# Recurrence stage of a two-block model: GpSimd operations in pieces, chain products on 128 rows, in-chunk products head by turn

## The chip, the cores and the metric

The kernel runs on one core of a Trainium2 chip. The metric is the device time of one execution in microseconds (us), the median of the runs shown. TensorE does the matrix products, VectorE and ScalarE elementwise work, GpSimd elementwise work between tiles in SBUF, and SyncE issues most transfers. Each engine takes its instructions strictly in the order in which the program lists them.

## The reference, cut to what matters

The whole model has two blocks. The stage that is changed computes the recurrence of the first block, 12 heads of 64 columns over 1024 tokens:

```python
def rwkv7_step(state, inp):
    r, decay, k, v, kk, a = inp
    sa = jnp.einsum('bhij,bhj->bhi', state, -kk)
    state = (state * decay[:, :, None, :]
             + sa[..., None] * (kk * a)[:, :, None, :]
             + v[..., None] * k[:, :, None, :])
    out = jnp.einsum('bhij,bhj->bhi', state, r)
    return state, out
...
_, y = lax.scan(rwkv7_step, state0, (r, decay, k, v, kk, a))
```

Before it, `x @ w_in` gives r, k and v. After it come a per-head normalization, a gate, the product with `w_out`, a mixture of 32 experts, and the second block with its attention.

## The kernel before

The scan is done in chunks of 64 tokens. The two heads of a pair lie in partitions 0 to 63 (`lo`) and 64 to 127 (`hi`). A *unit* is one pair and half of the sequence, so there are 12 units (`NU`) of 8 chunks (`HC`). Function `phase_units` works on them with these steps for each unit:

- `project`: 24 groups of three 128x512 products (lines 103 to 105). Each weight tile is first parted into a high and a low share: `wh` by ScalarE, `wl` by GpSimd (line 458, 128x1024).
- `tokens`: elementwise work that makes `G`, `BK`, `HK`; GpSimd takes lines 588 (128x512), 603 (64x512, twice) and 611 (128x1024); VectorE's lines 591 to 608 read two SBUF tiles each.
- `within`: the in-chunk products (line 636, K=64 rows, 128 columns), first all 8 chunks of the lo head, then all 8 of the hi head. VectorE masks the lo result straight from PSUM (line 642); for the hi head ScalarE copies (645) and GpSimd masks (647).
- `solve`: 15 small pairs of VectorE operations (706: a product of two SBUF tiles, 708: its sum).
- `masks`: GpSimd, line 722, four operations of 64x512. `inverse`: products on line 735, then `T64` (line 756).
- `chain`: the recurrence over the 8 chunks, in three steps a chunk. Step one: product with `G` and `X` (777), copied to `R` (768). Step two: `T64` by `R` (782), copied into `X` (768), and the first part of the output (785). Step three: the new state (789, 791) and the second part of the output, `H` by `X` (793). Each is issued for the lo and then for the hi head. 782 and 793 use 64 rows each (64*64 in the trace), 777, 785 and 789 use 128 rows (128*64).
- `finish`: normalization on GpSimd (815 to 844), transposes on TensorE (837).

The units overlap. Table `PLAN` gives, for each step of a unit, the slot in which it is emitted, 24 slots a unit; `ORDER` orders steps within one slot. So while the chain of unit v runs, `solve`, `masks` and `inverse` of unit v+1, `tokens` and `within` of unit v+2 and `project` of unit v+3 are emitted between its steps. Nothing reorders them later: a VectorE operation that takes long delays the chain's copies that are emitted behind it.

All results of TensorE go to PSUM tiles; `pA` has three buffers, `pC` one for each tag. The product on line 103 to 105 comes as one row in the trace; an f32 product of the chain comes as two rows (two passes).

Of the kernel before, what the change touches and what calls it, by code (L numbers as in the profile page):

```python
# [142 lines left out]
def phase_lowrank(g, xh0, xl0):  # L143
# [228 lines left out]
HC = 8  # L372
# [9 lines left out]
    "masks": [-21, -20, -19, -16, -16],  # L382
    "inverse": [-8, -7, -4, -3, -2, -2, 0, 0, 0],
    "start_state": [-12],
    "within": [-35, -35, -35, -35, -35, -34, -33, -33, -32, -31, -30],
    "tokens": [-47, -47, -46, -45, -44, -44, -43, -42, -41, -41, -40, -39, -38, -37, -37, -36, -34, -33, -33, -31,
        -31, -31, -29],
    "lt_load": [-24],
# [16 lines left out]
def phase_units(g, xh, xl):  # L405
    nc, tc, a = g.nc, g.tc, g.a
    with ExitStack() as c:
        wp = c.enter_context(tc.tile_pool(name="uw", bufs=2, reuse_waits="tile"))
        hv = c.enter_context(tc.tile_pool(name="uh", bufs=2, reuse_waits="tile"))
# [10 lines left out]
        lo, hi = slice(0, 64), slice(64, 128)  # L420
# [2 lines left out]
        nc.gpsimd.memset(T16, 0.0)  # L423

        L16, L32, T16T, X2 = (sm.tile([P, HC, 2, 64], F32, name=n) for n in ("L16", "L32", "T16T", "X2"))
        for t in (L16, L32, T16T, X2):
            nc.gpsimd.memset(t, 0.0)
        EP = el.tile([P, HC, 65], F32, name="EP")
        nc.gpsimd.memset(EP[:, :, 0:1], math.exp(-M0))
# [47 lines left out]
        M = {}  # L477
# [16 lines left out]
        def msplit2(j):  # L494
            if j < 12:
                mh, ml, m = M[j]
                kn = order[j][2]
                nc.gpsimd.tensor_tensor(ml[:, :kn], m[:, :kn], mh[:, :kn].bitcast(F32), op=OP.subtract)


        swap = {(1, 1): [(oload, 0, 0)], (1, 5): [(oload, 0, 2)], (2, 1): [(osplit, 0, 0)], (2, 2): [(osplit, 0, 1)],
# [48 lines left out]
        def tokens(v):  # L550
# [34 lines left out]
            fv = f[:, v, :, None]  # L585
            nc.vector.tensor_scalar(fv, EP[:, :, 64:65], math.exp(M0), None, op0=OP.mult)
            u.G = el.tile([P, HC, 2, 64], F32, name="G", bufs=2)
            nc.gpsimd.tensor_tensor(u.G[:, :, 1, :], w4(r), EP[:, :, 1:65], op=OP.mult)
            yield
            kn = el.tile([P, 512], F32, name="kn")  # L590
            nc.vector.scalar_tensor_tensor(kn, k, pc[:, 32 + q:33 + q], sq, op0=OP.mult, op1=OP.mult)
# [8 lines left out]

            u.BK = el.tile([P, HC, 2, 64], F32, name="BK")
            for sl, o in ((lo, 0), (hi, 1)):
                nc.gpsimd.tensor_tensor(u.BK[sl, :, o, :], w4(kn)[sl], w4(EN)[sl], op=OP.mult)
                nc.vector.tensor_tensor(u.BK[sl, :, 1 - o, :], w4(al)[sl], w4(EN)[sl], op=OP.mult)
                yield

# [4 lines left out]
            nc.gpsimd.tensor_tensor(u.HK, u.BK, fv[:, :, None, :].to_broadcast([P, HC, 2, 64]), op=OP.mult)  # L611
            yield
            pb = pA.tile([P, 512], F32, name="pA")
            nc.tensor.matmul(pb, ones, bo)
# [11 lines left out]
        def within(v):  # L626

            u = U[v]
            u.M = []
            for e, sl in enumerate((lo, hi)):  # L630
                M = el.tile([P, HC, 2, 64], F32, name=f"M{e}")
                for q in range(2):
                    pl = pA.tile([P, 4, 2, 64], F32, name="pA")
                    for i in range(4):
                        cc = 4 * q + i
                        nc.tensor.matmul(pl[:, i], u.BK[sl, cc], u.G[sl, cc])
                        if i == 1:
                            yield
                    qs = slice(4 * q, 4 * q + 4)
                    mb = mk.to_broadcast([P, 4, 2, 64])  # L640
                    if e == 0:
                        nc.vector.tensor_tensor(M[:, qs], pl, mb, op=OP.mult)
                        yield
                    else:
                        nc.scalar.activation(M[:, qs], pl, AF.Copy)
                        yield
                        nc.gpsimd.tensor_tensor(M[:, qs], M[:, qs], mb, op=OP.mult)
                u.M.append(M)
# [13 lines left out]
        def hand_over(v):  # L662

            u = U[v]
            h, q = divmod(v, NPAIR)
            u.L = sm.tile([P, HC, 64], F32, name="L")
            u.H = hv.tile([P, HC, 64], F32, name="H")
            u.GA, u.GB = (hv.tile([P, HC, 2, 64], F32, name=n) for n in ("GA", "GB"))
            u.XA, u.XB = (hv.tile([P, 2, HC, 64], F32, name=n) for n in ("XA", "XB"))
            MA, MB = u.M  # L670
            for s, M in ((lo, MA), (hi, MB)):
                nc.sync.dma_start(u.L[s], M[s, :, 0, :])
            for s, o, M, G, in ((lo, hi, MA, u.GA), (hi, lo, MB, u.GB)):
                nc.sync.dma_start(G[s], u.G[s])
                nc.sync.dma_start(G[o], M[o])
                nc.sync.dma_start(u.H[s], M[s, :, 1, :])
            yield
            u.TK = []
            for e, sl in enumerate((lo, hi)):
                pk = pA.tile([P, HC, 64], F32, name="pA")  # L680
                for cc in range(HC):
                    nc.tensor.transpose(pk[:, cc, :], u.HK[sl, cc], g.ident[sl, sl])
                    if cc == 3:
                        yield
                t = hv.tile([P, HC, 64], F32, name=f"TK{e}")
# [32 lines left out]
        def masks(v):  # L718
            u = U[v]
            for e, sl in enumerate((lo, hi)):  # L720
                for t, m in ((L16, "m16"), (L32, "m32")):
                    nc.gpsimd.tensor_tensor(t[sl, :, e, :], u.L[sl], cv(g, m)[sl][:, None, :].to_broadcast([64, HC, 64]), op=OP.mult)
                    yield

        def inverse(v):
# [26 lines left out]
            yield  # L752
            ps = pA.tile([P, HC, 64], F32, name="pA")
            yield from mul(ps, X2, T32T)
            u.T64 = hv.tile([P, HC, 64], F32, name="T64")
            nc.vector.tensor_tensor(u.T64, ps, T32T, op=OP.add)
            yield

        def chain(v):
# [12 lines left out]
            for cc in range(HC):  # L772
# [7 lines left out]
                for sl, G, X, TK, tag in hd:  # L780
                    us = pC.tile([P, 64], F32, name=tag)
                    nc.tensor.matmul(us[sl], u.T64[sl, cc, :], R[sl])
                    copy(sl, X[sl, 1, cc, :], us[sl])
                for sl, G, X, TK, tag in hd:
                    nc.tensor.matmul(yy[sl], G[:, cc, 1, :], X[:, 0, cc, :], start=True, stop=False)
# [1 line left out]
                for sl, G, X, TK, tag in hd:  # L787
# [2352 lines left out]
```

## Time and profile before

| | |
|---|---|
| median of 3 runs | 3401.09 us (3397.03 to 3405.79) |
| the profiled execution | 3407.47 us, span 3405.7 us |
| busy over the span | TensorE 89%, VectorE 64%, GpSimd 46%, ScalarE 45% |
| recurrence chains of the 12 units | from 260 to 912 us of the span |
| first expert weights requested | 951 us, behind this stage |

The profile is one execution. "Idle before" in its rows is the time in which the engine had nothing to do just before an operation, and the arrow names what ended it. [...]

### The profile page before, as it was taken

To read this page: it belongs to the slowest core of one execution; us is meant where nothing else is said; L and a number is where in the kernel's file an instruction comes from. 1 tells how busy PE (TensorE), PEld (TensorE's weight loads), DVE (VectorE), ACT (ScalarE), POOL (GpSimd) and SP (SyncE) were. 2 spreads that over 40 slices of the span, in tenths; PEclk is the share of its full clock that TensorE was granted. 3 is DMA by queue.
4 is the path that set the end of the run, shared out by engine and by line. 5 is a ranking of instruction groups with operands and counts; after the bars stand their busy time and mean duration, and the time that the engine had idled before them with its cause. 6 is when DMAs were issued, how large, how long until landed. Compare 5 with 4: busy or idle time off the path is not lost. (4 is left out here: it accounts for less than half of the span.)

```text
span 3405.7 us, 47172 instructions
## 1 busy us (share of the span) xinstructions
PE 3028.9 (89%) x16804; PEld 2114.5 (62%) x16804; DVE 2175.5 (64%) x3459; ACT 1535.0 (45%) x2828; POOL 1577.0 (46%) x1301
## 2 busy tenths in 40 slices
PE   7788888888978998699988988998899889999998
PEld 4365566565666765689864555557677665555556
DVE  2157787777468987768336666766447346667665
ACT  3343343333337977533224544445445334444452
POOL 0153555555344554554115554567546314444465
PEclk8888888888978999799999999999899989999999
DMA  9744453445579999532211111146224311111136
GB/s 298 279 111 103 107 146 93 110 109 151 156 253 312 323 329 336 184 112 83 91 63 51 39 47 44 37 144 209 92 75 158 123 52 58 41 49 41 41 106 213
DMA packets 394064, 457.14 MB, mean 134 GB/s; under 512 B 123319, under 2 KB 301970, under 8 KB 393698
## 3 DMA queue, kind: packets, MB, share of 16 engines
q1 hardware_dynamic: 380032, 426.15, 40.2%
q0 software_dynamic: 7616, 17.09, 1.5%
q10 hardware_dynamic: 6178, 10.86, 0.8%
q8 instruction: 133, 2.18, 0.3%
q14 instruction: 105, 0.86, 0.1%
HBM read 329.40 MB, written 101.11 MB: 126 GB/s over the span
## 5 line engine op out<-in xcount | busy, mean ns | idle before, releaser
L2110 ACT ACTIVATE p<-st 128x512 f32<-128x512 f32 (+1 forms) x672 | 378.2, 584 | 393.7 <-PE st L2108 313.0
L2029 DVE TENSOR_REDUCE mx<-s 128x1 f32<-128x1280 f32 x256 | 380.4, 1486 | 263.1 <-PE s L2028 263.1
L2120 POOL TENSOR_TENSOR acc<-acc,p 128x512 f32<-128x512 f32 x256 | 379.4, 1482 | 131.1 <-ACT p L2110 117.8
L2128 PE MATMUL o<-p,V 128*64 128x512 f32 (+1 forms) x1344 | 318.2, 595 | 0.0
L2120 DVE TENSOR_TENSOR acc<-acc,p 128x512 f32<-128x512 f32 x256 | 284.6, 1112 | 7.6
L1412 DVE TENSOR_TENSOR wl<-wr,wh 128x1024 fp32r<-128x1024 f32 x156 | 227.8, 1487 | 41.0 <-ACT wh L1411 40.9
L103 PE MATMUL pz<-xh,wh 128*128 128x512 f32 x440 | 229.1, 521 | 11.1 <-ACT wh L452 7.6
L1411 ACT ACTIVATE wh<-wr 128x1024 fp32r<-128x1024 f32 x192 | 198.9, 1055 | 40.9 <-DMA wr<-in_exp_up_dram 16.0
L105 PE MATMUL pz<-xh,wl 128*128 128x512 f32 x440 | 188.4, 428 | 11.5 <-POOL wl L458 7.9
L104 PE MATMUL pz<-xl,wh 128*128 128x512 f32 x440 | 187.8, 427 | 0.0
L103 PE MATMUL pj<-hh,wh 128*128 128x512 f32 (+1 forms) x416 | 160.6, 386 | 9.4 <-DVE xk L2780 4.6
L2128 PEld LDWEIGHTS o<-p,V 128*64 128x64 f32 x1344 | 81.7, 136 | 140.2 <-issue 136.4
L2120 POOL TENSOR_TENSOR acc<-p 128x512 f32<-128x512 f32 (+1 forms) x40 | 48.6, 1215 | 240.4 <-ACT p L2110 240.4
L1792 POOL TENSOR_TENSOR wl<-wr,wh 128x512 fp32r<-128x512 f32 (+1 forms) x70 | 88.4, 1275 | 152.5 <-ACT wh L1790 152.2
L105 PE MATMUL pj<-hh,wl 128*128 128x512 f32 (+1 forms) x416 | 156.6, 377 | 0.5 <-POOL wl L1792 0.5
L104 PE MATMUL pj<-hl,wh 128*128 128x512 f32 (+1 forms) x416 | 156.2, 376 | 0.0
L1412 POOL TENSOR_TENSOR wl<-wr,wh 128x1024 fp32r<-128x1024 f32 x36 | 88.8, 2470 | 145.5 <-ACT wh L1411 125.7
L2108 PE MATMUL st<-QQ,K 128*128 128x512 f32 (+1 forms) x352 | 150.5, 429 | 2.8 <-ACT p L2110 2.7
L2142 POOL TENSOR_TENSOR rg<-rg,gt 128x512 f32<-128x512 f32 (+1 forms) x40 | 48.5, 1213 | 221.3 <-ACT rg L2141 221.1
L105 PE MATMUL pj<-wh,hl 128*128 128x256 f32 x480 | 142.7, 297 | 4.6 <-POOL hl L1873 4.5
L104 PE MATMUL pj<-wl,hh 128*128 128x256 f32 x480 | 141.5, 295 | 4.5 <-DVE wl L1792 4.4
L103 PE MATMUL pj<-wh,hh 128*128 128x256 f32 x480 | 142.4, 297 | 1.2 <-DVE hh L1872 1.2
(515 smaller groups left out, 8415.9 us busy)
## 6 DMA issues: line engine op xcount, KB each, us to landing
wr<-in_exp_gate_dram SPq DMA_DIRECT2D x64, 512.0 KB
wr<-in_exp_up_dram SPq DMA_DIRECT2D x64, 512.0 KB
wr<-in_exp_down_dram SPq DMA_DIRECT2D x32, 1024.0 KB
w<-in_l_w_out_dram SPq DMA_DIRECT2D x56, 512.0 KB
wm<-in_l_w_mod_dram SPq DMA_DIRECT2D x48, 512.0 KB
w<-in_w_in_dram SPq DMA_DIRECT2D x40, 512.0 KB
wr<-in_l_w_in_dram SPq DMA_DIRECT2D x33, 512.0 KB
y<-ysd SPq DMA_DIRECT2D x16, 512.0 KB
```

The lines of the kernel that those rows point to most:

```text
L103: nc.tensor.matmul(out, lh, rh, start=start, stop=False)
L104: nc.tensor.matmul(out, lh, rl, start=False, stop=False)
L105: nc.tensor.matmul(out, ll, rh, start=False, stop=stop)
L1411: nc.scalar.activation(wh, w, AF.Copy)
L1412: eng.tensor_tensor(wl, w, wh.bitcast(F32), op=OP.subtract)
L1792: eng.tensor_tensor(st["l"][:, ks], st["w"][:, ks], st["h"][:, ks].bitcast(F32), op=OP.subtract)
L2029: nc.vector.tensor_reduce(m[:, j:j + 1], ps.rearrange("p a b -> p (a b)")[:, :SK], axis=AX.X, op=OP.max)
L2108: nc.tensor.matmul(st[:, :n], kk[:, kt * P:(kt + 1) * P], qv[:, pt.q0:pt.q0 + n], start=(j == 0), stop=(j == len(passes) - 1))
L2110: nc.scalar.activation(p[:, :n], st[:, :n], AF.Exp, scale=self.scale)
L2120: eng.tensor_tensor(a, r.p[r.kts[0], e][:, :n] if r.first else a, r.p[r.kts[i], e][:, :n], op=OP.add)
L2128: nc.tensor.matmul(pt.po[64 * e:64 * e + 64, :n], pt.out["V"](e, kt), r.p[kt, e][:, :n], start=(r.first and i == 0), stop=(r.last and i == ...
L2142: nc.gpsimd.tensor_tensor(rg[:, :n], rg[:, :n], pt.gt[:, :n], op=OP.mult)
```

## The change

The diff does three things. GpSimd's operations of lines 458, 498, 588, 603, 611 and 722 are cut along the free dimension into pieces of 256 elements a partition. `T64` and `H` become tiles of both heads, 128 rows by 2x64 columns a chunk, zero outside the head's own block, so that 782 and 793 run on all 128 rows with `R` or `X` whole; `T64` is one tile for all units, `H` is two in turn, and all three are cleared once at the start of the stage. And `within` issues the in-chunk products of the two heads in turn, with a PSUM tile for each; its part of `PLAN` is shortened to the steps that are left.

```diff
-    "within": [-35, -35, -35, -35, -35, -34, -33, -33, -32, -31, -30],
+    "within": [-35, -35, -35, -34, -33, -33, -32, -30],
...
-        for t in (L16, L32, T16T, X2):
+        T64, *Hs = (sm.tile([P, HC, 2, 64], F32, name=n) for n in ("T64", "H0", "H1"))
+        for t in (L16, L32, T16T, X2, T64, *Hs):
             nc.gpsimd.memset(t, 0.0)
...
-                nc.gpsimd.tensor_tensor(wl, w, wh.bitcast(F32), op=OP.subtract)
+                for c0 in range(0, KT, 2):
+                    nc.gpsimd.tensor_tensor(wl[:, c0:c0 + 2], w[:, c0:c0 + 2], wh[:, c0:c0 + 2].bitcast(F32), op=OP.subtract)
...
-            nc.gpsimd.tensor_tensor(u.G[:, :, 1, :], w4(r), EP[:, :, 1:65], op=OP.mult)
+            for c0 in range(0, HC, 4):
+                ks = slice(c0, c0 + 4)
+                nc.gpsimd.tensor_tensor(u.G[:, ks, 1, :], w4(r)[:, ks], EP[:, ks, 1:65], op=OP.mult)
...
-            u.M = []
-            for e, sl in enumerate((lo, hi)):
-                M = el.tile([P, HC, 2, 64], F32, name=f"M{e}")
-                for q in range(2):
-                    pl = pA.tile([P, 4, 2, 64], F32, name="pA")
-                    for i in range(4):
-                        cc = 4 * q + i
-                        nc.tensor.matmul(pl[:, i], u.BK[sl, cc], u.G[sl, cc])
-                        if i == 1:
-                            yield
...
+            u.M = [el.tile([P, HC, 2, 64], F32, name=f"M{e}") for e in range(2)]
+            for q in range(2):
+                pl = [pA.tile([P, 4, 2, 64], F32, name="pA") for _ in range(2)]
+                for i in range(4):
+                    cc = 4 * q + i
+                    for e, sl in enumerate((lo, hi)):
+                        nc.tensor.matmul(pl[e][:, i], u.BK[sl, cc], u.G[sl, cc])
+                    if i == 1:
                         yield
...
-            u.H = hv.tile([P, HC, 64], F32, name="H")
+            u.H = Hs[v % 2]
...
-                nc.sync.dma_start(u.H[s], M[s, :, 1, :])
+                nc.sync.dma_start(u.H[s, :, e, :], M[s, :, 1, :])
...
-                    nc.gpsimd.tensor_tensor(t[sl, :, e, :], u.L[sl], cv(g, m)[sl][:, None, :].to_broadcast([64, HC, 64]), op=OP.mult)
+                    for c0 in range(0, HC, 4):
+                        ks = slice(c0, c0 + 4)
+                        nc.gpsimd.tensor_tensor(t[sl, ks, e, :], u.L[sl, ks], cv(g, m)[sl][:, None, :].to_broadcast([64, 4, 64]), op=OP.mult)
...
-            u.T64 = hv.tile([P, HC, 64], F32, name="T64")
-            nc.vector.tensor_tensor(u.T64, ps, T32T, op=OP.add)
+            for e, sl in enumerate((lo, hi)):
+                nc.vector.tensor_tensor(T64[sl, :, e, :], ps[sl], T32T[sl], op=OP.add)
...
-                    nc.tensor.matmul(us[sl], u.T64[sl, cc, :], R[sl])
+                    nc.tensor.matmul(us[sl], T64[:, cc, e, :], R)
...
-                    nc.tensor.matmul(yy[sl], u.H[sl, cc, :], X[sl, 1, cc, :], start=False, stop=True)
+                for e, (sl, G, X, TK, tag) in enumerate(hd):
+                    nc.tensor.matmul(yy[sl], u.H[:, cc, e, :], X[:, 1, cc, :], start=False, stop=True)
```

Lines 603 and 611 are cut in the same way. The code grows by a few lines, so that line 458 is line 460 afterwards, 722 is 729, 636 is 644, 782 is 789 and 793 is 800.

In GpSimd's queue, in a unit from the middle of the stage, these rows stand behind the first half of the normalization before (`L_1114` and `L_1115` are the masked tiles L16 and L32, the row of `Y` is the second half of the normalization):

```order
L458 TENSOR_TENSOR wl<-w,wh 128x1024
L722 TENSOR_TENSOR L_1114<-L,const_102 64x8x64
L722 TENSOR_TENSOR L_1115<-L,const_102 64x8x64
L722 TENSOR_TENSOR L_1114<-L,const_102 64x8x64
L830 TENSOR_TENSOR Y<-Y,mv 128x512
L588 TENSOR_TENSOR G<-z_3118,EP 128x8x64
L458 TENSOR_TENSOR wl<-w,wh 128x1024
L722 TENSOR_TENSOR L_1115<-L,const_102 64x8x64
```

After the change the same place reads:

```order
L460 TENSOR_TENSOR wl<-w,wh 128x256 x4
L729 TENSOR_TENSOR L_1114<-L,const_102 64x4x64 x2
L729 TENSOR_TENSOR L_1115<-L,const_102 64x4x64 x2
L729 TENSOR_TENSOR L_1114<-L,const_102 64x4x64 x2
L837 TENSOR_TENSOR Y<-Y,mv 128x512
L593 TENSOR_TENSOR G<-z_3210,EP 128x4x64 x2
L460 TENSOR_TENSOR wl<-w,wh 128x256 x4
L729 TENSOR_TENSOR L_1115<-L,const_102 64x4x64 x2
```

No operation changed its place there; seven of the eight became pieces of half or a quarter of their size.

On TensorE, the in-chunk products of a unit (`pA_3923`, `pA_3929`: lo head, `pA_3936` and the tile behind it: hi head) stand among the chain's products like this before:

```order
L636 MATMUL pA_3923<-G_3798,BK_3897 128x128 x4
L636 MATMUL pA_3929<-G_3798,BK_3897 128x128 x4
L636 MATMUL pA_3936<-G_3798,BK_3897 128x128 x2
L782 MATMUL cA_3939<-R_3908,T64_3581 64x64
L782 MATMUL cB_3942<-R_3908,T64_3581 64x64
L785 MATMUL yy_3907<-XA_3055,GA_3053 64x64
L785 MATMUL yy_3907<-XB_3056,GB_3054 64x64
L636 MATMUL pA_3936<-G_3798,BK_3897 128x128 x2
```

and like this after it (`pA_4041` and `pA_4065` lo, `pA_4042` and `pA_4066` hi):

```order
L644 MATMUL pA_4041<-G_3908,BK_4012 128x128
L644 MATMUL pA_4042<-G_3908,BK_4012 128x128
L644 MATMUL pA_4041<-G_3908,BK_4012 128x128
L644 MATMUL pA_4042<-G_3908,BK_4012 128x128
L789 MATMUL cA_4053<-R_4025,T64_1118 64x64
L789 MATMUL cB_4056<-R_4025,T64_1118 64x64
L792 MATMUL yy_4024<-XA_3144,GA_3142 64x64
L792 MATMUL yy_4024<-XB_3145,GB_3143 64x64
L644 MATMUL pA_4065<-G_3908,BK_4012 128x128
L644 MATMUL pA_4066<-G_3908,BK_4012 128x128
```

The heads now alternate, eight products instead of ten stand ahead of this chain step, and the second pair of PSUM tiles is asked for while the first pair is being emptied. The chain's own products keep their places; `T64_1118` is the one tile of all units.

## Rows read from the trace of the kernel before

**Rows 1.** Busy time by window: us, then busy (and count) of each engine, PEclk, DMA

```profile
260.00:912.00 652.00, 566.26 (x4898) 389.50 (x4898) 477.72 (x1251) 243.59 (x445) 325.26 (x312) 0.89 0.45 118
870.00:912.00 42.00, 41.90 (x381) 27.45 (x380) 20.37 (x74) 11.99 (x24) 15.94 (x19) 1.00 0.36 113
```

**Rows 2.** Idle TensorE time before L782 and before L777: us, times

```profile
  DVE R L768: 73.2, 46
...
  DVE XA L791: 98.5, 43
```

**Rows 3.** TensorE in order of time, unit around 608: start us, us, what

```profile
608.09 0.47 PE L782 MATMUL cA<-R,T 64*64 64x64 f32 x2 [3.14 <-DVE R L768]
...
610.61 0.63 PE L103 MATMUL pz<-xh,wh 128*128 128x512 f32 x1
...
615.24 0.39 PE L103 MATMUL pz<-xh,wh 128*128 128x512 f32 x1
...
625.26 0.47 PE L777 MATMUL cA<-XA,GA 128*64 128x64 f32 x2 [3.79 <-DVE XA L791]
```

**Rows 4.** VectorE in order of time, the same stretch

```profile
602.91 2.22 DVE L706 TENSOR_TENSOR pr<-Tn,LT 64x9 f32<-64x9 f32 x1
...
606.58 1.00 DVE L706 TENSOR_TENSOR pr<-Tn,LT 64x25 f32<-64x25 f32 x1
...
607.82 0.22 DVE L768 COPY R<-cA 64x64 f32<-64x64 f32 x1
...
620.05 2.92 DVE L591 SCALAR_TENSOR_TENSOR kn<-z,pcol,sq 128x512 f32<-128x512 f32 x1
622.90 1.59 DVE L706 TENSOR_TENSOR pr<-Tn,LT 64x225 f32<-64x225 f32 x1
```

**Rows 5.** GpSimd in order of time, the same stretch

```profile
602.71 2.40 POOL L458 TENSOR_TENSOR wl<-w,wh 128x1024 fp32r<-128x1024 f32 x1 [3.01 <-ACT wh L452]
605.05 3.81 POOL L722 TENSOR_TENSOR L<-L,const 64x512 f32<-64x512 f32 x3
...
620.07 2.36 POOL L458 TENSOR_TENSOR wl<-w,wh 128x1024 fp32r<-128x1024 f32 x1
```

**Rows 6.** VectorE by line and shape, 260 to 912: busy us, mean ns, idle before

```profile
L591 DVE SCALAR_TENSOR_TENSOR kn<-z,pcol,sq 128x512 f32<-128x512 f32 x10 | 24.8, 2479 | 0.0
...
L756 DVE TENSOR_TENSOR T<-pA,T32T 128x512 f32<-128x512 f32 x12 | 8.3, 692 | 1.1 <-PE pA L735 0.8
...
L595 DVE SCALAR_TENSOR_TENSOR kn<-th,kn 128x512 f32<-128x512 f32 x10 | 6.9, 692 | 0.3
...
L706 DVE TENSOR_TENSOR pr<-Tn,LT 64x4 f32<-64x4 f32 x11 | 1.7, 158 | 0.4
```

**Rows 7.** TensorE, first passes of chain products around 478 and 481

```profile
478.81 0.27 PE L782 MATMUL cA<-R,T 64*64 64x64 f32 x1
...
479.07 0.27 PE L785 MATMUL yy<-XA,GA 128*64 128x64 f32 x1
...
481.28 0.22 PE L777 MATMUL cA<-XA,GA 128*64 128x64 f32 x1
...
481.40 0.65 PE L735 MATMUL pA<-X,T16T 128*64 128x64 f32 x16
```

**Rows 8.** TensorE, the first in-chunk products of one unit

```profile
634.44 2.16 PE L636 MATMUL pA<-G,BK 64*128 64x128 f32 x20
```

**Rows 9.** GpSimd by line and shape, 260 to 912

```profile
L458 POOL TENSOR_TENSOR wl<-w,wh 128x1024 fp32r<-128x1024 f32 x26 | 61.6, 2369 | 44.1 <-ACT wh L452 41.1 <-DMA L<-M 2.9
...
L843 POOL TENSOR_TENSOR yf<-yf,fbo 128x256 f32<-128x256 f32 x22 | 17.5, 797 | 40.5 <-issue 23.1 <-ACT yf L840 17.4
...
L815 POOL TENSOR_TENSOR mv<-st 128x8 f32<-128x8 f32 x11 | 2.7, 250 | 54.4 <-DVE st L798 54.4
```

**Rows 10.** ScalarE's copy of the second head's in-chunk products

```profile
L645 ACT ACTIVATE M<-pA 128x512 f32<-128x512 f32 x20 | 11.9, 597 | 36.8 <-PE pA L636 36.6
```

**Rows 11.** GpSimd at the start of the stage: the last large clear

```profile
163.84 0.94 POOL L427 MEMSET X<- 128x1024 f32 x1
```

More of the change, by code (lines that the diff above doesn't have):

```diff
@@ L497, in msplit2 @@
                 kn = order[j][2]
-                nc.gpsimd.tensor_tensor(ml[:, :kn], m[:, :kn], mh[:, :kn].bitcast(F32), op=OP.subtract)
+                for c0 in range(0, kn, 2):
+                    nc.gpsimd.tensor_tensor(ml[:, c0:c0 + 2], m[:, c0:c0 + 2], mh[:, c0:c0 + 2].bitcast(F32), op=OP.subtract)
         swap = {(1, 1): [(oload, 0, 0)], (1, 5): [(oload, 0, 2)], (2, 1): [(osplit, 0, 0)], (2, 2): [(osplit, 0, 1)],
@@ L602, in tokens @@
             for sl, o in ((lo, 0), (hi, 1)):
-                nc.gpsimd.tensor_tensor(u.BK[sl, :, o, :], w4(kn)[sl], w4(EN)[sl], op=OP.mult)
+                for c0 in range(0, HC, 4):
+                    ks = slice(c0, c0 + 4)
+                    nc.gpsimd.tensor_tensor(u.BK[sl, ks, o, :], w4(kn)[sl, ks], w4(EN)[sl, ks], op=OP.mult)
                 nc.vector.tensor_tensor(u.BK[sl, :, 1 - o, :], w4(al)[sl], w4(EN)[sl], op=OP.mult)
@@ L610, in tokens @@
             u.HK = el.tile([P, HC, 2, 64], F32, name="HK")
-            nc.gpsimd.tensor_tensor(u.HK, u.BK, fv[:, :, None, :].to_broadcast([P, HC, 2, 64]), op=OP.mult)
+            for c0 in range(0, HC, 2):
+                ks = slice(c0, c0 + 2)
+                nc.gpsimd.tensor_tensor(u.HK[:, ks], u.BK[:, ks], fv[:, ks, None, :].to_broadcast([P, 2, 2, 64]), op=OP.mult)
             yield
@@ L628, in within @@
             u = U[v]
-            u.M = []
-            for e, sl in enumerate((lo, hi)):
-                M = el.tile([P, HC, 2, 64], F32, name=f"M{e}")
-                for q in range(2):
-                    pl = pA.tile([P, 4, 2, 64], F32, name="pA")
-                    for i in range(4):
-                        cc = 4 * q + i
-                        nc.tensor.matmul(pl[:, i], u.BK[sl, cc], u.G[sl, cc])
-                        if i == 1:
-                            yield
[L639 to L642, printed above, removed]
-                        yield
[L644 to L648, printed above, removed]
+            u.M = [el.tile([P, HC, 2, 64], F32, name=f"M{e}") for e in range(2)]
[6 more added lines that the diff above has]
+                    if i == 1:
+                        yield
+                qs = slice(4 * q, 4 * q + 4)
+                mb = mk.to_broadcast([P, 4, 2, 64])
+                nc.vector.tensor_tensor(u.M[0][:, qs], pl[0], mb, op=OP.mult)
+                yield
+                nc.scalar.activation(u.M[1][:, qs], pl[1], AF.Copy)
+                yield
+                nc.gpsimd.tensor_tensor(u.M[1][:, qs], u.M[1][:, qs], mb, op=OP.mult)
             yield
@@ L672, in hand_over @@
                 nc.sync.dma_start(u.L[s], M[s, :, 0, :])
-            for s, o, M, G, in ((lo, hi, MA, u.GA), (hi, lo, MB, u.GB)):
+            for e, s, o, M, G in ((0, lo, hi, MA, u.GA), (1, hi, lo, MB, u.GB)):
                 nc.sync.dma_start(G[s], u.G[s])
                 nc.sync.dma_start(G[o], M[o])
-                nc.sync.dma_start(u.H[s], M[s, :, 1, :])
+                nc.sync.dma_start(u.H[s, :, e, :], M[s, :, 1, :])
             yield
@@ L721, in masks @@
                 for t, m in ((L16, "m16"), (L32, "m32")):
-                    nc.gpsimd.tensor_tensor(t[sl, :, e, :], u.L[sl], cv(g, m)[sl][:, None, :].to_broadcast([64, HC, 64]), op=OP.mult)
+                    for c0 in range(0, HC, 4):
+                        ks = slice(c0, c0 + 4)
+                        nc.gpsimd.tensor_tensor(t[sl, ks, e, :], u.L[sl, ks], cv(g, m)[sl][:, None, :].to_broadcast([64, 4, 64]), op=OP.mult)
                     yield
@@ L779, in chain @@
                 yield
-                for sl, G, X, TK, tag in hd:
+                for e, (sl, G, X, TK, tag) in enumerate(hd):
                     us = pC.tile([P, 64], F32, name=tag)
-                    nc.tensor.matmul(us[sl], u.T64[sl, cc, :], R[sl])
+                    nc.tensor.matmul(us[sl], T64[:, cc, e, :], R)
                     copy(sl, X[sl, 1, cc, :], us[sl])
@@ L791, in chain @@
                     nc.vector.scalar_tensor_tensor(dst, X[sl, 0, cc, :], f[sl, v, cc:cc + 1], sp[sl], op0=OP.mult, op1=OP.add)
-                for sl, G, X, TK, tag in hd:
-                    nc.tensor.matmul(yy[sl], u.H[sl, cc, :], X[sl, 1, cc, :], start=False, stop=True)
+                for e, (sl, G, X, TK, tag) in enumerate(hd):
+                    nc.tensor.matmul(yy[sl], u.H[:, cc, e, :], X[:, 1, cc, :], start=False, stop=True)
                 nc.scalar.activation(u.Y[:, cc, :], yy, AF.Copy)
```

## The prediction

> **What bounds the stage now.** I read the busy time by windows first. The chains of the 12 units fill the 652 us from 260 to 912, so a unit takes 54.3 us. In them TensorE is busy 566.26 us and stands idle 85.7 us, 7.1 us a unit, and its mean granted clock is 0.89; in the last 42 us of the stage, where it hardly idles, the clock is 1.00 [rows 1]. A clock of 0.89 costs (1 - 0.89) x 54.3 = 6.0 us of full-speed work a unit. What is left, 54.3 - 7.1 - 6.0 = 41.2 us, is TensorE's work at full clock. So TensorE bounds the stage, but 13 of 54 us are lost beside its work.
>
> Who makes it wait is in the view by line. Nearly all the time that TensorE stands before 782 ended with VectorE's copy into R, and before 777 with VectorE's new state XA: 73.2 and 98.5 us [rows 2] (these sums count weight loads and products apart, so they exceed the 85.7 us). The timeline shows two large stalls a unit, 3.14 us before a 782 and 3.79 us before a 777 [rows 3]; I count 10 units with both, since the last two have no later unit left to prepare between their chain steps. Behind the first the 128x512 products are recorded with 0.63 us (610.61) and later with 0.39 us (615.24) [rows 3]: the lower clock follows the stall.
>
> Why VectorE is late: behind the stall at 608.09 stand operations that should be short. A product of 64x9 elements took 2.22 us, one of 64x25 took 1.00 us, and the copy to R came only at 607.82 [rows 4]. A 64x4 product takes 0.158 us in the mean [rows 6]. The 2.22 us end at 605.13, just when GpSimd's weight split (602.71 + 2.40 = 605.11) ends; the 1.00 us end at 607.58, where the second of GpSimd's three masks (3.81 us for three from 605.05) ends [rows 4, 5]. The second stall has the same picture: line 591 takes 2.92 us from 620.05 and ends behind GpSimd's split of 620.07 + 2.36 = 622.43, and the 64x225 product takes 1.59 us [rows 4, 5]. In the mean 591 takes 2.479 us, the same kind of operation on line 595 takes 0.692 [rows 6]. So a VectorE operation that reads two SBUF tiles waits until the GpSimd operation under way has ended, and gets in at its end.
>
> **The change part by part**, for a unit.
>
> Pieces. A split of 128x1024 takes 2.369 us [rows 9]; a quarter by elements alone is 0.59 us, which I take as the longest single wait, 0.6. The nearest row of the same shape, 843, shows 0.797 with its own waits in it [rows 9]; that is the upper bound. First stall: three small products (2.22 and 1.00 us shown, and one between them that I put at 1.0 by the same pattern) last 4.2 us; with pieces each can wait 0.6 and then runs for 0.15 to 0.2, and part of the first wait has passed, so about 1.9 together. Gain 2.3 us of 3.14. Bounds: 0 (VectorE does not get in between pieces) and 2.6 (each waits half a piece). Second stall: 591 falls from 2.92 to 0.69 + 0.6 = 1.3, the 64x225 product from 1.59 to about 1.1. Gain 1.8 of 3.79 us; bounds 0 and 2.3. What is late next: the rest of VectorE's own work that is emitted ahead of those copies; so 0.8 and 2.0 us of the stalls stay.
>
> Clock. Of the 6.0 us I give back 40%, 2.4 us, because the stalls shrink and do not vanish. Bounds 0 and 5.
>
> Chain on 128 rows. Between the starts of 782 and 785, which differ in shape (64*64, then 128*64), lie 0.26 us; between 777 and 735, both 128*64, lie 0.12 us for the same four passes [rows 7]. The change of shape costs 0.14 us. With T64 and H on 128 rows the change between 782 and 785 and that between 789 and 793 go: 2 x 8 x 0.14 = 2.24 us. Part of it lies where VectorE sets the pace; I take 1.8. Bounds 0 and 2.24. The columns are the same 64, so no more time for the products themselves.
>
> In-chunk products by turns. 20 passes take from 634.44 to 636.52, 0.104 us each [rows 8], so 32 passes 3.3 us. Passes of two heads on different rows can run together, as the two heads of 782 do (0.26 us for four passes with the change of shape) [rows 7]. If they pair, 1.65 us go; I take 1.3. Bounds: 0 and 1.65.
>
> What it adds. VectorE writes T64 in two operations of 512 elements instead of one: 0.692 us more [rows 6], just ahead of the unit's first 782, so on the path: 0.7. Both products of 782 now wait for both copies to R: 0.1 in the mean, since only a stalled 782 notices it (one copy is 0.22 [rows 4]). The second pair of PSUM tiles in `within` waits for ScalarE's copy of the first, 0.597 us [rows 10], with a chain step between them as cover: 0.4. Sum 1.2. GpSimd gets 19 more instructions a unit (9 for three splits, 4 masks, 2, 1 and 3 for lines 603, 588 and 611). It is busy 325.26 of 652 us [rows 1], so half of its time covers them. The bound of the price is the [128x8] operation of 815, 0.250 us [rows 9]: 19 x 0.25 = 4.8 us if nothing covered it. At the start, three more clears of 0.94 us [rows 11] delay the first split by 2.8 us; in return the first products need only its first quarter, 1.75 us earlier, so 1 us is lost there. The first two units' in-chunk products, ahead of the chain, give some 4 us back.
>
> Sum for a unit: -2.3 - 1.8 - 2.4 - 1.8 - 1.3 + 1.2 = -8.4 us; for 10 units -84, with the two ends -3: -87 us. All that follows waits for the stage's end (the expert weights are requested behind it), so the whole time moves. 3407.5 - 87 = 3320 for an execution like the profiled one; it lies 6.4 us above the median of the runs, so 3314 for the median.
>
> The sum holds together with the clock: full-speed work 41.2 - 1.8 - 1.3 = 38.1, idle 7.1 - 4.1 + 1.2 = 4.2, together 42.3 us; in 45.9 us that is a mean clock of 0.92.
>
> **The rivals.**
>
> 1. The forecast, all three parts work in part: chance 0.60, range 3255 to 3350. With every term at its upper bound it is -2.6 - 2.3 - 5 - 2.24 - 1.65 + 1.2 = -12.6 us a unit, -126 - 3, about 3272; two more units would make 3247.
>
> 2. The pieces do not let VectorE in, because GpSimd's next piece is always queued: then only TensorE's terms remain, -1.8 - 1.3 + 1.2 = -1.9 a unit, -22 in all, 3379. For it: four pieces wait for nothing between them. Against: three masks of 64x512 stood back to back in just that way, and a VectorE product ended at each boundary [rows 4, 5]. Chance 0.15.
>
> 3. GpSimd's fixed cost comes onto the path, where its lines 603 and 588 feed the in-chunk products: 19 x 0.2 = 3.8 us a unit against -8.4, so -46 - 3, 3352. For it: small operations show that such a cost exists [rows 9]. Against: GpSimd is idle half the time [rows 1]. [...] Chance of this rival 0.10.
>
> 4. The clock, slower than before. The change takes activity from TensorE; if that holds the clock down for longer, a unit takes 42.3 / c. At c = 0.78 that is 54.2, the time of before; below it the kernel is slower. At 0.75: 56.4, +2.1 a unit, +21, 3422. For it: lower clock stands behind every long stall now. Against: with hardly any idle time it is 1.00 [rows 1], and the idle time shrinks too. Chance 0.08.
>
> 5. No change: the two stalls move to other waits of the same length, 3390 to 3411. Chance 0.07.
>
> **How the numbers follow.** The likeliest case gives 3314. The range reaches to rivals 2 and 3 and to the upper bounds: 3258 to 3380; outside it are rival 4, rival 5 and a little of the first. This kernel's runs differ by up to 0.26%, so 0.3%, 10 us, is about what can be told. Faster: 0.60 + 0.15 + 0.10 = 0.85; same 0.07; slower 0.08.
>
> **What would show it.** In the profile after: 591 near 1.3 us in the mean instead of 2.5, no small product on 706 over 1 us; the stalls before 782 and 777 at about 0.8 and 2.0 us; a mean clock of some 0.92 in the stage; 0.12 us between 782 and 785; a pair of in-chunk passes in the time of one; units of about 46 us. Wrong would be: VectorE products that still end only with a whole run of pieces (rival 2), idle TensorE time that ends with GpSimd (3), or a lower mean clock with fewer stalls (4).

## The result and the profile after

The changed kernel takes 3352.97 us (median of 4 runs, 3349.82 to 3354.52) against 3403.44 for the kernel before (4 runs, 3397.03 to 3412.60): a ratio of 0.9844, 95% interval 0.9822 to 0.9867. It is faster, as forecast, and inside the range; but 50 us were won where the sum gave 87. The profiled execution (3354.52 us, span 3352.7) is 53.0 us under the one of before, and its chains, from 265.6 to 863.9 us, are 52.8 us shorter (598.3 against 651.1 us). The stage begins with GpSimd's first clear, at 160.7 us before and at 167.8 after; from there to the first chain product 97.8 us pass, 99.3 before. Ahead of that clear the two executions differ by +7.1 us and behind the chains by -5.8 us, in work that the change leaves as it was. So the difference lies in the stage; a unit (mean of units 3 to 9) went from 56.0 to 50.8 us, where 46 was forecast.

The first view is the busy time by window, with the columns of [rows 1] (PEclk is the mean clock granted to TensorE, as a share of full speed), over the chains of the kernel before and of the changed kernel:

```profile
260.00:911.10 651.10, 565.36 (x4895) 388.77 (x4894) 476.88 (x1248) 243.37 (x444) 325.26 (x312) 0.89 0.45 118
...
265.60:863.90 598.30, 521.29 (x4894) 357.95 (x4894) 451.92 (x1259) 244.37 (x444) 363.71 (x524) 0.91 0.49 128
```

TensorE's busy time fell from 565.36 us to 521.29, by 44.1 us, but its idle time only from 85.7 to 77.0, by 8.7. The forecast let 2.9 us of idle time a unit go, 29 us for its 10 units.

Who ends the idle time now is in the view by line over the same stretch: the engine, the line with the operation and shape, count, then busy us and mean ns, then idle before and its releaser. Before, the same view (which counts products alone, where [rows 2] add the weight loads) had these rows, and nothing ahead of `cB` of 782:

```profile
L782 PE MATMUL cA<-R,T 64*64 64x64 f32 x192 | 33.5, 258 | 32.0 <-DVE R L768 28.3 <-DVE T L756 2.7
...
L789 PE MATMUL cA<-XA,TK 128*64 128x64 f32 x192 | 32.9, 257 | 7.5 <-DVE XA L768 7.5
L777 PE MATMUL cA<-XA,GA 128*64 128x64 f32 x192 | 32.8, 255 | 45.9 <-DVE XA L791 45.8
```

After:

```profile
L789 PE MATMUL cB<-R,T 128*64 128x64 f32 x192 | 34.0, 263 | 4.5 <-DVE T L763 4.5
L789 PE MATMUL cA<-R,T 128*64 128x64 f32 x192 | 33.9, 262 | 20.9 <-DVE R L775 17.2 <-DVE T L763 2.7
...
L784 PE MATMUL cA<-XA,GA 128*64 128x64 f32 x192 | 32.4, 252 | 43.6 <-DVE XA L798 43.6
L796 PE MATMUL cA<-XA,TK 128*64 128x64 f32 x192 | 32.3, 253 | 4.7 <-DVE XA L775 4.7
```

(784 is 777 of before, 789 is 782, 796 is 789, 775 is 768.) The wait for R fell, the wait for the state XA hardly, and a new one stands ahead of the second head's product: it ends with line 763, which writes T64.

In order of time, a unit shows where. TensorE's rows, to be read against [rows 3]:

```profile
576.47 0.27 PE L789 MATMUL cA<-R,T 128*64 128x64 f32 x1 [0.70 <-DVE R L775]
...
582.18 0.33 PE L784 MATMUL cA<-XA,GA 128*64 128x64 f32 x2 [1.00 <-DVE XA L798]
...
585.13 0.37 PE L789 MATMUL cA<-R,T 128*64 128x64 f32 x1 [0.71 <-DVE R L775]
...
586.97 0.63 PE L104 MATMUL pz<-xl,wh 128*128 128x512 f32 x1
```

In this unit the stalls of 3.14 and 3.79 us are gone; waits of 0.7 to 1.0 us stand in a row, and the lower clock still follows them: PEclk is 0.50 from 587 to 589 us, and the long product takes 0.63 us, where one at 577.19, with PEclk at 1.00 from 576 to 579 us, takes 0.39. In the mean over units 0.90 and 1.65 us stay at the two places (the table of steps below), where 0.8 and 2.0 were forecast. VectorE and GpSimd in the same stretch, to be read against [rows 4, 5]:

```profile
573.86 0.42 DVE L711 TENSOR_TENSOR pr<-Tn,LT 64x9 f32<-64x9 f32 x1
...
574.51 0.48 DVE L711 TENSOR_TENSOR pr<-Tn,LT 64x16 f32<-64x16 f32 x1
...
575.22 0.48 DVE L711 TENSOR_TENSOR pr<-Tn,LT 64x25 f32<-64x25 f32 x1
...
575.94 0.22 DVE L775 COPY R<-cA 64x64 f32<-64x64 f32 x1
...
577.35 0.44 DVE L711 TENSOR_TENSOR pr<-Tn,LT 64x36 f32<-64x36 f32 x1
...
578.76 0.46 DVE L711 TENSOR_TENSOR pr<-Tn,LT 64x64 f32<-64x64 f32 x1
```

```profile
573.51 2.82 POOL L460 TENSOR_TENSOR wl<-w,wh 128x256 fp32r<-128x256 f32 x4 [3.43 <-ACT wh L453]
576.29 4.37 POOL L729 TENSOR_TENSOR L<-L,const 64x256 f32<-64x256 f32 x6
```

The 64x9 product that waited for a whole split (2.22 us) takes 0.42 now. But GpSimd's pieces stand without a gap from 573.51 to 580.66, and the products under them take 0.42 to 0.54 us. No product waits long, and nearly all wait a little: the 64x36 product takes 0.44 us, where it took 0.22 before, at a time when GpSimd stood idle:

```profile
609.12 0.22 DVE L706 TENSOR_TENSOR pr<-Tn,LT 64x36 f32<-64x36 f32 x1
```

The means by line and shape say the same as [rows 6] did for before: line 596 (591 before) is at 1.24 us, as forecast, from 2.48.

```profile
L596 DVE SCALAR_TENSOR_TENSOR kn<-z,pcol,sq 128x512 f32<-128x512 f32 x10 | 12.4, 1236 | 0.0
```

The two TensorE terms are seen in the passes, to be read against [rows 7, 8]:

```profile
549.10 1.16 PE L644 MATMUL pA<-G,BK 64*128 64x128 f32 x16
...
559.87 0.27 PE L789 MATMUL cA<-R,T 128*64 128x64 f32 x1
...
560.03 0.22 PE L792 MATMUL yy<-XA,GA 128*64 128x64 f32 x1
```

16 in-chunk passes start within 1.09 us (the next product starts at 550.19), 0.068 us each where it was 0.104. Pass by pass the trace has them in pairs 7 ns apart and the pairs 0.112 us apart, the distance of single passes before: a pair does take the time of one. The saving is less than half because the last eight of the 20 passes of [rows 8] overlapped in part already, at the seam between the heads. Between the starts of 789 and 792 lie 0.16 us, where it was 0.26 with the change of shape and 0.12 was forecast.

### The profile page after: what moved, and what is told of

It reads as the page before. It is cut to its first block, busy times and chain, and to the rows that moved or that the text cites. A ratio compares the mean times of both kernels' runs of the same rounds, so it can differ in the third digit from the quotient of the medians.

```text
span 3352.7 us, 47462 instructions
## 1 busy us (share of the span) xinstructions
PE 2974.5 (89%) x16804; PEld 2080.9 (62%) x16804; DVE 2149.2 (64%) x3471; ACT 1537.0 (46%) x2828; POOL 1623.5 (48%) x1564
## 5 line engine op out<-in xcount | busy, mean ns | idle before, releaser
L105 PE MATMUL pz<-xh,wl 128*128 128x512 f32 x440 | 184.6, 420 | 15.9 <-POOL wl L460 10.2
```

The lines of the kernel that those rows point to most:

```text
L105: nc.tensor.matmul(out, ll, rh, start=False, stop=stop)
```

## The experiments

Chains below means the stretch from the first chain product to the last of the profiled execution; idle, busy and clock are TensorE's in it, by the busy time by window. Each ratio is to the kernel before on the same chip (its medians: 3410.56 for the first four kernels, 3407.10 for the next four, 3408.90 for the next three, 3412.09 for the last).

| kernel | median us | ratio, 95% interval | chains us | idle | busy | clock |
|---|---|---|---|---|---|---|
| before | 3403.44 | | 651.1 | 85.7 | 565.4 | 0.89 |
| changed | 3352.97 | 0.9844 (0.9822 to 0.9867) | 598.3 | 77.0 | 521.3 | 0.91 |
| pieces alone | 3364.71 | 0.9864 (0.9844 to 0.9885) | 608.2 | 51.3 | 556.9 | 0.92 |
| 128 rows alone | 3420.53 | 1.0031 (1.0019 to 1.0043) | 652.5 | 111.1 | 541.4 | 0.89 |
| turns alone | 3395.81 | 0.9961 (0.9947 to 0.9975) | 640.9 | 89.6 | 551.4 | 0.89 |
| pieces and turns | 3350.32 | 0.9835 (0.9812 to 0.9857) | 601.9 | 53.6 | 548.3 | 0.91 |
| changed, R apart | 3350.23 | 0.9828 (0.9805 to 0.9851) | 595.3 | 67.6 | 527.8 | 0.91 |
| R apart, dense T64 | 3338.65 | 0.9795 (0.9772 to 0.9817) | 585.3 | 60.4 | 524.9 | 0.91 |
| the same, halves | 3367.83 | 0.9874 (0.9855 to 0.9894) | 615.4 | 86.7 | 528.7 | 0.89 |
| the same, eighths | 3331.21 | 0.9768 (0.9749 to 0.9786) | 571.9 | 58.3 | 513.6 | 0.94 |
| the same, late solve | 3352.30 | 0.9844 (0.9817 to 0.9870) | 598.9 | 77.3 | 521.6 | 0.92 |
| pieces, turns, spread solve | 3378.23 | 0.9908 (0.9887 to 0.9929) | 634.8 | 71.8 | 563.0 | 0.88 |
| changed, no splits | 3335.88 | 0.9787 (0.9771 to 0.9804) | 584.1 | 65.4 | 518.7 | 0.92 |
| changed, no splits, no masks | 3308.68 | 0.9712 (0.9695 to 0.9729) | 561.6 | 54.1 | 507.5 | 0.96 |

The last four columns come from one execution of each kernel, and the executions of one kernel differ: the whole time of the kernel with dense T64 lies between 3335.50 and 3345.40 us, with a mean clock of 0.947 to 0.937 over the span, and its profiled execution is the slowest of the five; that of pieces and turns (3344.06 us) is the fastest of its five. How much of this lies in the chains is not known, so differences of a few us between chains are not shown to be more than that.

Where in a unit the idle time lies is worked out from the trace: a step runs from one group of chain products (G, T64, state) to the next, 24 to a unit, and takes the idle time ahead of all TensorE's instructions in it; the mean is over units 3 to 9. Steps 4 and 9 are the two stalls of [rows 3]. The steps left out have at most 0.31 us each, but for 10 and 11 of the spread solve (0.99 and 0.58).

```
step                       1     4     6     7     8     9    12    14    18   unit
before                  0.10  2.77  0.26  0.13  0.54  3.24  0.00  0.05  0.57   7.67
pieces alone            0.09  0.39  0.71  0.51  0.22  1.56  0.00  0.10  0.57   4.16
128 rows alone          0.51  3.21  0.36  0.12  0.58  3.37  0.00  0.81  0.84   9.79
changed                 0.50  0.90  1.00  0.65  0.29  1.65  0.06  0.19  0.87   6.48
R apart, dense T64      0.11  0.64  0.87  0.32  0.25  1.37  0.13  0.15  0.87   5.08
the same, halves        0.12  2.10  0.36  0.24  0.88  2.12  0.13  0.20  0.87   7.29
the same, eighths       0.12  0.41  0.60  0.41  0.58  1.13  0.09  0.15  0.87   4.90
the same, late solve    0.11  0.64  1.03  0.38  0.00  0.18  2.57  0.00  0.87   6.20
spread solve            0.10  0.00  0.00  0.04  0.00  0.52  2.45  0.23  0.42   5.61
no splits, no masks     0.50  0.05  0.00  0.26  0.67  0.83  0.98  0.00  0.87   4.58
```

**Each part alone.** The theory, A: the pieces cut the two stalls, but other operations of VectorE now meet a piece. Its rivals: VectorE's own work is the limit (B), or GpSimd's cost for each instruction is on the path (C). The first three kernels are the kernel before with one part of the change each; their edits are the pieces, the chain and `within` parts of the diff above.

Pieces alone:

> The kernel before with GpSimd's operations in pieces and nothing else. Theory A (the waits are spread): the stalls of steps 4 and 9 of a unit (2.77 and 3.24 us before) shrink to about 1 and 1.7 us as they do with the whole change, but other VectorE operations now meet a piece, and idle time comes up in steps 1, 6 and 7: about -2.5 us a unit with the clock, 3375 us. Rival B (VectorE's own work is the limit once nothing holds it): the same, but VectorE's operations of steps 6 and 7 are no longer than before. Rival C (GpSimd's cost for each instruction is on the path): under 1 us a unit is won, 3392 to 3405 us, and idle time of TensorE ends with GpSimd.

Measured: 46 us faster. The idle time of steps 4 and 9 fell by 4.06 us, which is what the forecast gave for the two stalls (4.1); steps 6 and 7 took 0.83 back. All of TensorE's idle time in the chains still ends with VectorE (by line 12.3 us before 782, 35.1 before 777 and 4.0 before 789). B and A differ little here; C is out.

128 rows alone:

> The kernel before with the chain products of T64 and H on 128 rows and nothing else. By the changes of shape in the trace after (0.16 instead of 0.26 us, twice a chunk for a unit of 8 chunks) 1.6 us of full-speed work go, and T64 in two operations gives 0.7 back: -1 us a unit, 3391 us. If the stalls take up what TensorE saves (it waits for VectorE anyway) there is nothing: 3400. By the forecast's own terms (1.8 less 0.8): 3391.

Measured: 10 us slower, where 10 us faster or nothing was expected. TensorE's busy time fell by 24.0 us and its idle time rose by 25.4. By line, over the chains (before: 32.0, nothing, 45.9, 7.5, as above):

```profile
L783 PE MATMUL cB<-R,T 128*64 128x64 f32 x192 | 33.9, 262 | 4.7 <-DVE T L757 4.7
L783 PE MATMUL cA<-R,T 128*64 128x64 f32 x192 | 33.9, 262 | 39.2 <-DVE R L769 35.5 <-DVE T L757 2.7
L778 PE MATMUL cB<-XB,GB 128*64 128x64 f32 x192 | 33.9, 262 | 0.0
L778 PE MATMUL cA<-XA,GA 128*64 128x64 f32 x192 | 33.4, 259 | 54.3 <-DVE XA L792 54.3
L790 PE MATMUL cB<-XB,TK 128*64 128x64 f32 x192 | 32.6, 254 | 0.0
L790 PE MATMUL cA<-XA,TK 128*64 128x64 f32 x192 | 32.3, 252 | 12.9 <-DVE XA L769 12.8
```

Every wait of the chain for VectorE is longer, and the chains are 1.4 us longer in all. Most of the 10 us lies at the start: from GpSimd's first clear to the first chain product 106.1 us pass, 99.3 before. The clears there, in the profile of this kernel:

```profile
163.89 0.53 POOL L423 MEMSET T<- 128x512 f32 x1 [155.17 <-DMA gtp<-gt]
167.02 1.84 POOL L428 MEMSET L<- 128x1024 f32 x2 [2.60 <-DMA gtp<-gt]
...
170.59 0.94 POOL L428 MEMSET T<- 128x1024 f32 x1
171.49 1.83 POOL L428 MEMSET H<- 128x1024 f32 x2
```

The three new clears cost the 2.8 us of the forecast, and the clear ahead of them also waits 2.60 us for a transfer of the stage before; before, and in the kernel with pieces alone, it waits for none. I take it that the larger pool of tiles reaches into memory that this transfer still reads. That was not tried by itself; in the kernel with dense T64 below, which has no cleared T64 tile, no clear behind the first waits for a transfer.

Turns alone:

> The kernel before with the in-chunk products head by turn and nothing else. 16 passes took 1.09 us after and 1.66 before: 1.1 us a unit for 32 passes, less a wait for the PSUM tiles: about -1 us a unit, 3391 us, if TensorE's work counts; nothing, 3400, if the wait for ScalarE's copy takes it back. By the forecast (1.3 less 0.4): 3392.

Measured: 15 us by the medians, 10.2 us in the chains; busy time fell by 14.0 us, and idle time rose by 3.9, of which 2.5 end with ScalarE's copy. As forecast (0.9 a unit).

**The changed kernel without rows, and with rows that cost less.** Pieces and turns without the 128 rows:

> The changed kernel without the chain products on 128 rows. If the three parts add up as they did alone (-46, +10, -15 us): 3410 - 61, so 10 us faster than the whole change, about 3345 us. Rival, the forecast's view (the rows are worth 1.0 us a unit in the whole, once the stalls are small): slower than the whole change, about 3363.

Measured: 0.9835 against 0.9844, which is the same within the intervals, where one expectation had 10 us less than the whole change and the other some 8 more; in the chains the rows win 3.6 us, and at the start (97.8 us from first clear to chain against 91.6) they lose 6.2. TensorE's busy time is 27.0 us shorter with them, its idle time 23.4 us longer. Two kernels take the rows' costs away one by one. R apart:

```diff
+        R = [sm.tile([P, 64], F32, name=f"R{e}") for e in range(2)]
+        for t in R:
+            nc.gpsimd.memset(t, 0.0)
...
-                    copy(sl, R[sl], ry[sl])
+                    copy(sl, R[e][sl], ry[sl])
...
-                    nc.tensor.matmul(us[sl], T64[:, cc, e, :], R)
+                    nc.tensor.matmul(us[sl], T64[:, cc, e, :], R[e])
```

> The changed kernel with R as a tile for each head, zero in the other head's rows, so that a product of T64 waits for its own head's copy alone; T64 is still written in two operations. If the wait for both copies is what ate the rows' gain (idle time before G's product rose from 0.57 to 0.87 us in step 18, and likewise in steps 4 and 14), 0.8 us a unit comes back: about 3347 us where the whole change has 3355. Rival: T64's second operation and the clears are the price, and this changes nothing: 3355.

Measured: 3.0 us less in the chains, where 8 were expected; by the medians it can't be told from the changed kernel. The idle time ahead of the first head's product that ended with R fell from 17.2 to 11.3 us, as the second row shows, and all idle time fell by 9.4 us; but TensorE's busy time, with the same products, rose by 6.5. So the wait for both copies is there, and little of it is seen in the time; why the busy time rose is open.

```profile
L791 PE MATMUL cB<-R,T 128*64 128x64 f32 x192 | 33.8, 261 | 4.7 <-DVE T L766 4.7
L791 PE MATMUL cA<-R,T 128*64 128x64 f32 x192 | 33.7, 260 | 13.9 <-DVE R L778 11.3 <-DVE T L766 1.7
```

Dense T64: since R is zero in the other head's rows, T64 needs no zeros, so one VectorE operation writes it again and one clear goes:

```diff
-            for e, sl in enumerate((lo, hi)):
-                nc.vector.tensor_tensor(T64[sl, :, e, :], ps[sl], T32T[sl], op=OP.add)
+            u.T64 = hv.tile([P, HC, 64], F32, name="T64")
+            nc.vector.tensor_tensor(u.T64, ps, T32T, op=OP.add)
...
+                    nc.tensor.matmul(us[sl], u.T64[:, cc, :], R[e])
```

> As the one with R apart, and T64 is dense again (one VectorE operation, no clear): 128 rows without either cost. Step 1 of a unit loses its 0.6 us again: 1.4 us a unit together, 14 us, about 3340 us, and less than pieces and turns without rows. Rival: TensorE's saving of 0.1 us a change of shape is worth nothing, since the chain waits for VectorE: then it stands with pieces and turns alone, about 3345 to 3350.

Measured: 3338.65 us, as expected, and 10.0 us less in the chains than with R apart alone. Step 1 has its 0.11 us back, and by line:

```profile
L791 PE MATMUL cB<-R,T 128*64 128x64 f32 x192 | 34.0, 263 | 0.0
L791 PE MATMUL cA<-R,T 128*64 128x64 f32 x192 | 33.7, 260 | 13.8 <-DVE R L778 11.2 <-DVE T L766 1.7
```

So the rows alone are worth 16.6 us in the chains (601.9 to 585.3), 1.4 a unit: the forecast's 1.8 was near. By the medians, with the clears at the start, it is 11.7 us. T64's second operation took 10.0 of the 16.6, and 9.3 of these lie in step 1 of the 12 units; the 3.0 us for the wait for both copies are too few to be told apart.

**What is left of the stalls.** GpSimd's work taken away from the changed kernel, first the splits, then the masks of line 729 too. These kernels leave out work, as their expectations say.

```diff
-                for c0 in range(0, KT, 2):
-                    nc.gpsimd.tensor_tensor(wl[:, c0:c0 + 2], w[:, c0:c0 + 2], wh[:, c0:c0 + 2].bitcast(F32), op=OP.subtract)
+                pass
```

> The changed kernel, with GpSimd's weight splits of this stage left out (the low share of the weights is a tile of zeros, so the low products add nothing). Theory A: GpSimd's pieces still hold VectorE; without the splits (a third of its work of the stage) the small products fall from 0.4 to under 0.3 us and a unit's idle time from 6.5 to about 4: 3320 us. Rival B: VectorE's own work sets the pace in steps 4 to 9, so idle time stays above 5.5 us a unit and the time at 3340 to 3353. Rival C: as much as A, but TensorE's waits that vanish are those that end with GpSimd.

> The changed kernel with GpSimd's weight splits and its masks for the inverse left out (zeros in their place), so that hardly anything of GpSimd stands against the solve. Theory A (pieces still hold VectorE): the small products fall to 0.2 to 0.3 us, idle time goes from 5.4 us a unit without splits to about 3: 3315 us. Rival B (VectorE's own work): idle time stays above 4.5 us and the time near 3333.

Measured: 11.6 us of idle time go with the splits and 11.3 more with the masks, and the chains are 14.2 and 36.7 us shorter. A 64x16 product takes 0.51, 0.43 and 0.26 us in the three kernels. In steps 4 to 9 the idle time falls from 4.49 to 1.81 us a unit (step 12 takes 0.9 of it back): some 60% of what the pieces leave there is still GpSimd holding VectorE. I take the rest for VectorE's own work, though GpSimd is still busy for 191.3 us of these chains with what was not left out, so its share can be larger. With the splits gone the time lies between A and B; with both gone it is below A's 3315, while the idle time of the unit (4.58) is B's. Neither theory alone fits.

**The size of a piece**, on the kernel with dense T64:

> The kernel with dense T64 and R apart, with GpSimd's operations in half as many pieces of twice the size. If the longest single wait for a piece sets the stalls, steps 4 and 9 get about 0.6 us each back and the small products go from 0.4 to 0.6 us: +1 us a unit or more, 3350 us. If the cost of each of GpSimd's instructions were on the path (rival C), fewer would be faster: 3330. If neither, 3338.

> The kernel with dense T64 and R apart, with GpSimd's operations in twice as many pieces of half the size (128 elements a partition). If shorter waits go on paying as from halves to quarters (30 us in the chains), though less, since VectorE's own work stays: steps 4 and 9 lose 0.5 to 0.7 us more, 3325 us. Rival: GpSimd's cost for each instruction (its busy time rose from 330 to 380 us with the quarters) now keeps it busy under most of VectorE's operations, or makes the low share of the weights late: 3345 us or slower, with TensorE waiting for line wl.

The three kernels by line and shape, VectorE, with halves, quarters and eighths:

```profile
L714 DVE TENSOR_TENSOR pr<-Tn,LT 64x9 f32<-64x9 f32 x11 | 8.7, 788 | 0.4
...
L714 DVE TENSOR_TENSOR pr<-Tn,LT 64x9 f32<-64x9 f32 x11 | 4.6, 420 | 0.4
...
L714 DVE TENSOR_TENSOR pr<-Tn,LT 64x9 f32<-64x9 f32 x11 | 2.2, 198 | 0.4
```

(Line 498, whose splits stand at the end of the stage, kept its quarters in all three.) Measured: halves cost 30.1 us in the chains: 2.8 us of idle time a unit at steps 4, 8 and 9, of which steps 6 and 7 give 0.6 back. Eighths win 13.4 more, though by the ratios the last step isn't told apart with certainty. GpSimd's busy time goes from 337.6 over 366.6 to 427.5 us and TensorE does not wait for it: C is out once more. And the wait gets shorter with the piece: the 64x9 product takes 0.788, 0.420 and 0.198 us in the mean. Why a VectorE operation waits for the rest of GpSimd's is not shown.

**VectorE's work moved out of steps 4 to 9.** The solve over 11 slots, or its last two products in step 10:

```diff
-    "solve": [-22, -22, -22, -22, -22, -20, -20, -20, -20, -20, -20, -19, -18, -18, -17, -17],
+    "solve": [-22, -21, -21, -20, -19, -19, -18, -17, -16, -15, -15, -14, -14, -13, -13, -12],
```

```diff
+    "solve": [-22, -22, -22, -22, -22, -20, -20, -20, -20, -20, -20, -19, -18, -14, -14, -14],
```

> The same kernel with the 16 solve steps spread over 11 slots (-22 to -12) instead of 6 (-22 to -17). If VectorE's own work in steps 2 to 9 of a unit sets the pace there (it is busy 96 to 100% of steps 6 to 9, and 40 to 90% of steps 10 to 23), idle time falls by about 1.5 us a unit and with it the clock's loss: 3345 - 25 = 3320 us. Rival: the waits only move with the solve to other steps, or the solve ends too late for the inverse: 3345 or slower.

> The kernel with dense T64 and R apart, with the last two products of the solve (and its store) emitted in step 10 (-14) instead of steps 6 and 7. Theory A and B together (VectorE, held by pieces and by its own work, is the limit in steps 4 to 9 and has room in step 10, which lasts 3.2 us with 2.2 us of VectorE's work): idle time falls by 1 to 1.5 us a unit, 3338 - 15 = 3323 us. Rival: as with the spread solve they meet the pieces of line BK in steps 10 to 12 and the wait stands there: 3338 or slower.

Measured: both are slower than the kernel that they were made from, by 32.9 and 13.6 us in the chains (by the ratios the late solve only just). Steps 4 to 9 lose 2.8 and 1.2 us of idle time a unit, but step 12 gets 2.5: the rivals were right. One such place of the late solve, VectorE and then TensorE:

```profile
539.82 1.01 DVE L714 TENSOR_TENSOR pr<-Tn,LT 64x196 f32<-64x196 f32 x1
...
541.25 0.59 DVE L714 TENSOR_TENSOR pr<-Tn,LT 64x225 f32<-64x225 f32 x1
...
542.29 0.75 DVE L521 SCALAR_TENSOR_TENSOR z<-pz,pcol,z 128x511 f32<-128x511 f32 x1
...
543.57 0.26 DVE L800 SCALAR_TENSOR_TENSOR XA<-XA,f,cA 64x64 f32<-64x64 f32 x1
```

```profile
543.89 0.33 PE L786 MATMUL cA<-XA,GA 128*64 128x64 f32 x2 [2.38 <-DVE XA L800]
```

The products moved are emitted ahead of the chain's state (line 800), and with the `tokens` operations already there they make a new queue of 3.75 us (539.82 to 543.57) in front of it.

## Why the prediction was right, and what was mis-sized

The direction and the mechanism held: VectorE operations that read two SBUF tiles end with GpSimd's operations (the 64x9 product of 2.22 us with the split, [rows 4, 5]), pieces let them in sooner (0.42 us for that product after, 1.24 for line 596 in the mean instead of 2.48), and the whole time follows the stage (53.0 us less in the profiled executions, 52.8 in the chains). That the time lies in the range says little of this, since the range reaches over rivals 2 and 3; what shows it is the kernel with the pieces alone (46 of the 50 us) and the size of the piece. The sum was 34 us too large against the profiled execution (53.0 won, not 87). By its own terms, over the chains:

- **The two stalls**, -41: steps 4 and 9 gave 4.06 us a unit with the pieces alone, the 4.1 of the forecast. What it lacked was the next wait: steps 6 and 7 got 0.83 us, and the idle time fell by 34.4 us. The forecast saw that something is late next and put it into the 0.8 and 2.0 us that stay in the same stalls, not into other steps.
- **Clock**, -24: the term that was off most. With the pieces alone the mean clock rose to 0.92, as forecast, and (1 - clock) x chains fell from 71.7 to 51.2 us, by 20.5. But TensorE's busy time, with the same products, fell by 8.5 us only. The forecast took (1 - clock) x time as work lost beside the idle time; part of the low clock lies in the idle time itself and was counted twice. By the trace's clock over the idle stretches alone that is 9.5 us before and 4.5 with the pieces. Of the 15.5 us that are missing, then, 3.5 are a clock that rose less, 5.0 stood in the idle time, and 7.0 stay open.
- **Chain on 128 rows**, -18: measured -16.6 once its costs are gone. A change of shape costs 0.10 us (0.26 less 0.16), not 0.14.
- **Its costs**, +8 for T64 and R: measured +13.0 (10.0 and 3.0, the second too small to be sure of). T64's second operation stands ahead of a unit's chain, where nothing covers it, and step 1 is 0.7 us longer in units 3 to 9, as the term said (1.69 us with two operations, 0.97 with one); but it is longer in all 12 units, where the sum counted 10, and by 1.4 us in unit 10.
- **In-chunk products by turns**, -13 + 4: measured -10.2. The 0.104 us a pass were a mean over passes that in part overlapped already; single passes lie 0.112 us apart.
- **The ends**, -3: measured -1.5. The first split began 10.6 us after the first clear, 5.0 before: 5.6 us later, where 2.8 were forecast.

Of the gap of 34 us, then, pieces and clock make 22 (65 forecast, 42.9 measured); the rows with their costs make 6 in the changed kernel (10 forecast, 3.6 over pieces and turns), the turns some 3 where they stand with the pieces (6.3 won there), the ends 1.5.

The rivals: rival 3 named 3352, the time that came, but for a reason that did not. Its price was right (GpSimd's busy time rose by 38.5 us for 212 instructions more, 0.18 us each, where it said 0.2), its place was not: 74.8 of the 77.0 us of TensorE's idle time end with VectorE, 2.2 with ScalarE, none with GpSimd. Rival 2 is out by line 596 (1.24 us), rival 4 by the clock, rival 5 by the time.

The lowest ratio of a kernel here that does all the work is that with dense T64 and eighths: 3331.21 us, 0.9768 against 0.9844 for the change as it was made.

## What to carry to other kernels

If an engine waits for another's whole instruction, cut the instruction that holds, and try smaller pieces while the holder has idle time (here halves to quarters paid clearly, 30.1 us in the chains, quarters to eighths less, 13.4, and not with certainty); then look which operations wait a little that waited for nothing before. Work taken from the engine that is waiting (here TensorE's passes) is worth only what the waits do not take back (128 rows alone: 24.0 us less of busy time, 25.4 more of idle time), so an edit that saves there but adds even one operation ahead of the chain on the engine that is late can lose. And count a lower clock from busy time alone, beside the idle time (pieces alone: 20.5 us by the clock over the whole chains, 8.5 by TensorE's busy time).

## What was not expected of the hardware

In these single executions the mean clock did not follow the idle time. The late solve has 77.3 us of idle time in the chains and a clock of 0.92, the dense kernel 60.4 us and 0.91, the spread solve 71.8 us and 0.88. Executions of one kernel differ too (dense T64: 0.937 to 0.947 over the span), so it is not shown that the kernels do, and which stalls bring the lower clock was not settled.

The cost of a change of shape can be read in the profiles of before and after: 0.26 us from the start of a product of 64 rows to that of one of 128 rows (478.81 to 479.07, [rows 7]), 0.16 between two of 128 rows in the chain (559.87 to 560.03), so 0.10 us for the change. What TensorE does in this time is not shown.
